# Grouped attention of a two-layer trunk: probabilities times values in float32r parts, both heads in one operand

## The chip, the core and the metric

One core of a Trainium2 chip runs the whole program. The metric is the time of one execution in microseconds on the device, lower is better. The engines are TensorE (PE, with its weight loads as PEld), VectorE (DVE), ScalarE (ACT), GpSimd (POOL, nearly unused here) and SyncE (SP), which issues the DMAs.

## The reference

The program is one inference step of a trunk of two layers, for 128 context tokens and 512 latent tokens (640 in all, five tiles of 128). Each layer has a grouped attention (8 query heads, 2 key heads), a state space branch (S5), a neighbourhood attention, gates that merge the three, and a gated MLP. The part that the change touches is the product of probabilities and values in the grouped attention:

```
s = jnp.einsum('bqgrd,bkgd->bgrqk', q_i, k).astype(jnp.float32) * scale
p = jax.nn.softmax(s, axis=-1).astype(v.dtype)
return jnp.einsum('bgrqk,bkgd->bqgrd', p, v)
```

A latent token attends to 512 latent keys and 128 cached ones (640 keys, five tiles), a context token to the 128 context keys (one tile). All of it is in float32.

## The kernel before

**Two kinds of product.** Nearly all large products are made from float32r parts: an operand x is split into hi (x rounded to float32r, by ACT) and lo (x - hi, by DVE; the helper is `split`, lines 130 and 99), and hi·hi, hi·lo and lo·hi are added up in PSUM. The weights are such a stream of hi/lo tiles (`raw`, `hi`, `lo`). A few products, among them probabilities times values, take plain float32 operands.

**Grouped attention.** `gqa` runs over four pairs of heads p; `stack` transposes the queries of the pair and splits them into `qst`; then `gqa_unit` runs for the token tiles t = 1, 2, 3, 4, 0. A unit computes the scores of both heads (`scores`, PSUM tiles `sc`: 8 products of 320 columns for t > 0), the softmax (`softmax`: on DVE the maximum `mx`, the reciprocal `rc` and the scaling of `P`; on ACT the exponential), transposes P tile by tile (`transpose_P`: up to four 128x128 transposes into one PSUM tile `tp`, copied by ACT into `PT`), and multiplies by the values (`pv`): for each key tile and head a float32 product with the 64 value columns as stationary operand and 128 probabilities columns as moving one; the two heads go into column tiles, that is output partitions 0 to 63 and 64 to 127 of one PSUM tile `y`. ACT copies `y` into `ya`. The PSUM tiles of `tp` (named `PT`, `y` or `tp` in rows) are a ring of two. A unit with t > 0 has 10 transposes and 10 such products, one with t = 0 has 2 and 2: 168 of each in a layer. The profile shows every float32 product of this kind as two records.

**What stands around it.** In the mixer of a layer the order of program text is: S5 input, S5 scan (`s5_scan`, marked as high priority, 64 dependent steps on DVE in tiles `sx` and `a`), projections, `gqa`, then a number of gate projections (`gates`; 14 items in layer 0 and 12 in layer 1, `AHEAD`), then `s5_out` in eight steps, each followed by a gate item. A step of `s5_out` needs the state after the scan: ACT copies it into `HK`, and PE multiplies (`mm<-HK,v` and `mm<-U,v`). After it come `glu` (tiles `a`), branch and output projections. A scheduler reorders this text at build time by its own estimate of times; on each engine the resulting order is fixed, and the engine executes it in that order. So the gate products (`mm<-h,hi` and `mm<-h,lo`) stand between the products of the attention. `s5_out` and the gates share a ring of two PSUM tiles `mm`, so that not more than the gates in front of a step and half a gate item behind it can be computed before that step has its state.

Lines in rows: 227 is every matmul, 230 every transpose, 130 every ACT operation, 99 every DVE operation with two tensors, 112 and 117 DVE operations with scalars, 852 and 856 the maximum and the reciprocal of the softmax.

Of the kernel before, what the change touches and what calls it, by code (L numbers as in the profile page):

```python
# [10 lines left out]
F = mybir.dt.float32  # L11
R = mybir.dt.float32r
# [38 lines left out]
class Trunk:  # L51
# [621 lines left out]
    def mixer(self, l):  # L673
        with ExitStack() as ey:
            p_y = self.pool(ey, "y")
            with ExitStack() as ek, ExitStack() as ec:
                p_z = self.pool(ek, "z")
                zt = p_z.tile([128, 5, NT], F, tag="zt", name="zt")
                va = p_z.tile([128, 6, 128], F, tag="va", name="va")
                HS = self.slot_a([128, 82, 2, 32])  # L680
                U = self.slot_v().rearrange("p a (b c) -> p a b c", c=80)
                self.run_all(self.zu(l, U))
# [85 lines left out]
    def zqkv(self, l, zt, va):  # L768
        def copy(t, dst, src):
            if t % 2:  # L770
                self.cpy(dst, src)
            else:
                self.act(dst, src)

        def ev_q(t, o):
            copy(t, zt[:, t, 0:512], o)

        def ev_kv(t, o):
            self.act(zt[:, t, 512:640], o[:, 0:128])
            copy(t, va[:, t], o[:, 128:256])  # L780
            if t == 0:
                self.dma(self.O["ga_v"][l], va[:, 0])

        self.dma(va[:, 5], self.A["cva"][l])
        return self.tm_run("zq", l, 2, 512, ev_q), self.tm_run("zkv", l, 4, 256, ev_kv)

    def nv(self, l, VN):
# [45 lines left out]
    def transpose_P(self, parts, pool, npt):  # L833

        pt = []
        for g in range(0, len(parts), 4):
            n = len(parts[g:g + 4])
            tp = self.tp("PT")
            for i, x in enumerate(parts[g:g + 4]):
                self.transpose(tp[:, i * 128:i * 128 + 128], x)  # L840
            sb = pool.tile([128, 512], F, tag="PT", name="PT", bufs=npt)
            self.act(sb[:, :n * 128], tp[:, :n * 128])
            pt.extend(sb[:, i * 128:i * 128 + 128] for i in range(n))
        return pt

    def softmax(self, P, src, nk):

# [100 lines left out]
    def gqa_unit(self, pool, p_sc, p, t, q, va):  # L948

        kv = p // 2  # L950
        k, klo = self.kst[:, kv], self.kst[:, 2 + kv]
        nk = 640 if t else 128
        qv = lambda x: x[:, t * 128:t * 128 + 128]
        sc = []
        for hh in range(2):
            sc.append(p_sc.tile([128, 1024], F, tag="sc", name="sc"))
            for a, c0, n in ((0, 128, 320), (512, 448, 320)) if t else ((0, 0, 128),):
                self.scores(sc[hh][:, a:a + n], q[:, hh], k, klo, qv, lambda x: x[:, c0:c0 + n])
        P = pool.tile([128, 2, 640], F, tag="P", name="P", bufs=2)
        self.softmax(P, [x.rearrange("p (b c) -> p b c", b=2)[:, :, :320] if t else x[:, :128] for x in sc], nk)  # L960
        pt = self.transpose_P([P[:, hh, kt * 128:kt * 128 + 128] for kt in range(nk // 128) for hh in range(2)], pool, 2)
        o = self.pv([1, 2, 3, 4, 5] if t else [0], pt, lambda vt, hh: va[:, vt, kv * 64:kv * 64 + 64])
        c = t * 128
        self.act(self.ya[:, p, c:c + 128], o[:, 0:128])


    def neighbourhood(self, l, p_na, p_y, Ga):
# [623 lines left out]
```

## Time and profile before

| What | Value |
|---|---|
| median of 3 runs | 2423.01 us (2422.66 to 2423.14) |
| the profiled execution | 2418.54 us, of which the span of the core is 2416.8 us |
| PE busy | 2334.5 us, 97% of the span |
| PE weight loads busy | 2103.6 us, 87% |
| DVE busy | 1501.8 us, 62% |
| ACT busy | 1221.7 us, 51% |
| share of PE, DMA, ACT and DVE in the chain that ended last | 85%, 4%, 4%, 3% |
| mean granted TensorE clock | 0.99 of full speed |

The busy shares are means over the whole program. Where an engine waits, and for what, is read from the stretches around the grouped attention: in layer 0 it runs from 221 to 458 us and in layer 1 from 1430 to 1673 us.

### The profile page before, as it was taken

The page shows a single profiled execution, that of the slowest core. Times are in us where ns is not written, and L with a number is a line of the kernel's source. Part 1 is how long each engine was busy: PE and PEld are TensorE (multiplying, and loading weights), DVE is VectorE, ACT ScalarE, POOL GpSimd, SP SyncE. Part 2 cuts the span into 40 slices and gives each one's busy share as a digit, 9 for nine tenths or more (in the row PEclk, how much of TensorE's full clock was granted, in tenths as well). Part 3 has the DMA queues.
Part 4 walks back from the last instruction along what each step waited for, and adds up shares of the span by engine and source line. Part 5 has one row for each costly group of instructions (what it writes and reads, how often), then busy time and mean ns, then how long its engine had stood idle before and what let it go on. Part 6 is the DMA issues. An engine that isn't in the chain of part 4 may idle for free.

```text
span 2416.8 us, 41307 instructions
## 1 busy us (share of the span) xinstructions
PE 2334.5 (97%) x16026; PEld 2103.6 (87%) x16026; DVE 1501.8 (62%) x3339; ACT 1221.7 (51%) x2657; POOL 0.7 (0%) x6
## 2 busy tenths in 40 slices
PE   5999999998999999999999999999999999999998
PEld 4899898877887899999888998888998899999886
DVE  8789647366557776665474495463775665444456
ACT  5434676336536444344364447754474564444444
POOL 0000000000000000000000000000000000000000
PEclk8999999999999999999999999999999999999999
DMA  7863242444244666654555323413321532222335
GB/s 270 276 220 98 100 147 68 161 147 132 80 157 159 204 200 208 201 173 138 170 183 186 121 81 124 138 49 124 97 64 54 176 130 71 79 72 78 114 114 174
DMA packets 160270, 334.56 MB, mean 138 GB/s; under 512 B 39434, under 2 KB 73290, under 8 KB 160074
## 3 DMA queue, kind: packets, MB, share of 16 engines
q1 hardware_dynamic: 160074, 331.92, 41.7%
q8 instruction: 126, 2.06, 0.4%
q14 instruction: 70, 0.57, 0.1%
HBM read 288.71 MB, written 52.53 MB: 141 GB/s over the span
## 4 chain that ended last, share of the span: by engine, by line
PE 85%; DMA 4%; ACT 4%; DVE 3%; issue 1%; SPq 0%; DVEq 0%; ACTq 0%
PE mm L227 49%; PE m L227 16%; PE mx L227 7%; PE tq L227 4%; PE y L227 3%; PE PT L230 2%; DMA ar<-in_wmod 2%; PE sc L227 1%; DMA raw<-in_wst 1%; ACT HK L130 1%; DVE lo L99 1%; PE BT L230 1%; ACT h L130 1%; PE E L227 1%; DMA cd<-pr 1%
## 5 line engine op out<-in xcount | busy, mean ns | idle before, releaser
L227 PE MATMUL mm<-h,hi 128*128 128x384 f32 (+1 forms) x3808 | 855.8, 313 | 6.3 <-ACT h L130 4.1
L227 PEld LDWEIGHTS mm<-h,hi 128*128 128x128 f32 x3808 | 642.7, 190 | 23.4 <-issue 12.8
L227 PE MATMUL mm<-h,lo 128*128 128x384 f32 (+1 forms) x1904 | 593.7, 312 | 0.0
L99 DVE TENSOR_TENSOR lo<-raw,hi 128x1024 fp32r<-128x1024 f32 x294 | 359.6, 1224 | 294.2 <-ACT hi L130 282.6
L130 ACT ACTIVATE hi<-raw 128x1024 fp32r<-128x1024 f32 x294 | 310.9, 1058 | 291.5 <-PE mm L227 196.6
L227 PEld LDWEIGHTS mm<-h,lo 128*128 128x128 f32 x1904 | 361.5, 190 | 5.2 <-issue 4.9
L227 PE MATMUL m<-h,hi 128*128 128x256 f32 (+1 forms) x1120 | 250.6, 312 | 2.1 <-ACT vn L130 1.1
L227 PEld LDWEIGHTS m<-h,hi 128*128 128x128 f32 x1120 | 188.7, 190 | 7.8 <-issue 4.4
L227 PE MATMUL m<-h,lo 128*128 128x256 f32 (+1 forms) x560 | 174.0, 311 | 0.1
L117 DVE SCALAR_TENSOR_TENSOR c<-u,blob,c 128x641 f32<-128x641 f32 x156 | 137.9, 884 | 2.2
L130 ACT ACTIVATE PT<-PT 128x512 f32<-128x512 f32 (+1 forms) x176 | 86.8, 498 | 93.1 <-PE PT L230 72.9
L227 PEld LDWEIGHTS m<-h,lo 128*128 128x128 f32 x560 | 106.2, 190 | 1.8 <-issue 1.4
L130 ACT ACTIVATE u<-mm 128x256 f32<-128x256 f32 (+1 forms) x156 | 48.0, 344 | 117.0 <-PE mm L227 117.0
L227 PE MATMUL mm<-a,hi 128*128 128x384 f32 (+1 forms) x384 | 89.3, 320 | 4.2 <-ACT a L130 3.1
L130 ACT ACTIVATE HK<-a 64x32 f32<-64x32 f32 (+1 forms) x256 | 77.5, 337 | 8.2 <-PE mm L227 6.2
L227 PE MATMUL mm<-hi,sph 128*128 128x512 f32 x208 | 78.6, 393 | 1.5 <-ACT sph L130 1.4
L227 PE MATMUL mm<-lo,sph 128*128 128x512 f32 x208 | 78.5, 392 | 0.0
L99 DVE TENSOR_TENSOR pr<-PW,cS 128x576 f32<-128x576 f32 x64 | 47.9, 755 | 48.3 <-PE mx L227 32.3
L227 PE MATMUL mm<-set,hi 128*128 128x384 f32 (+1 forms) x324 | 74.8, 317 | 0.5 <-DVE a L117 0.4
L227 PE MATMUL mm<-hi,spl 128*128 128x512 f32 x208 | 73.2, 393 | 0.0
L130 ACT ACTIVATE c<-u,blob 128x641 f32<-128x641 f32 x78 | 72.2, 925 | 1.9
L227 PEld LDWEIGHTS mm<-a,hi 128*128 128x128 f32 x384 | 63.9, 190 | 7.5 <-ACT a L130 4.1
(357 smaller groups left out, 4295.3 us busy)
## 6 DMA issues: line engine op xcount, KB each, us to landing
raw<-in_wst SPq DMA_DIRECT2D x308, 512.0 KB, 3.7
ar<-in_wmod SPq DMA_DIRECT2D x80, 512.0 KB, 4.0
cd<-pr SPq DMA_DIRECT2D x32, 288.0 KB, 4.4
v<-cd SPq DMA_DIRECT2D x32, 288.0 KB
wm<-in_wmod SPq DMA_DIRECT2D x8, 1024.0 KB
xd<-xt SPq DMA_DIRECT2D x15, 512.0 KB, 2.8
xt<-xd SPq DMA_DIRECT2D x15, 512.0 KB, 6.0
bd<-BT SPq DMA_DIRECT2D x28, 256.0 KB, 3.7
```

The costliest lines, as they stand in the source:

```text
L99: return self.nc.vector.tensor_tensor(out=out, in0=a, in1=b, op=op)
L117: self.nc.vector.scalar_tensor_tensor(out=out, in0=a, scalar=s, in1=b, op0=op0, op1=op1)
L130: return self.nc.scalar.activation(out=out, in_=a, func=func, **kw)
L227: return self.nc.tensor.matmul(out=out, lhsT=lhsT, rhs=rhs, start=start, stop=stop)
L230: return self.nc.tensor.transpose(out, in_, self.ident)
```

## The change

The values are kept as (hi | lo) pairs: for each token tile and key head a stationary operand of 128 columns, 64 of hi and 64 of lo. The probabilities of both heads are transposed as before, but the PSUM tile is now split into hi (ACT, in the place of the copy) and lo (DVE, new), each 128x512 (or 128x256 for the last key tile). Per key tile there are two products: the stationary operand with hi of both heads (256 columns), and the same with lo. The result has hi·p in partitions 0 to 63 and lo·p in 64 to 127; ACT copies the second half out (`yl`), and DVE adds the two halves into `ya`, once per head. The products of a group of key tiles are issued one group of transposes late. The neighbourhood attention keeps the old form.

```diff
-                va = p_z.tile([128, 6, 128], F, tag="va", name="va")
+                va = p_z.tile([128, 6, 2, 128], R, tag="va", name="va")
...
-            copy(t, va[:, t], o[:, 128:256])
+            put_v(t, o[:, 128:256])
             if t == 0:
-                self.dma(self.O["ga_v"][l], va[:, 0])
-
-        self.dma(va[:, 5], self.A["cva"][l])
+                self.act(v32, o[:, 128:256])
+                self.dma(self.O["ga_v"][l], v32)
+
+        def put_v(t, src):
+            v = src.rearrange("p (a d) -> p a d", a=2)
+            self.split(va[:, t, :, 0:64], va[:, t, :, 64:128], v)
+
+        v32, cva = (self.p_st.tile([128, 128], F, tag=x, name=x, bufs=1) for x in ("v32", "cva"))
+        self.dma(cva, self.A["cva"][l])
+        put_v(5, cva)
...
+    def pv_pair(self, P, nk, tiles, pool, v):
+        n, todo, o = nk // 128, [], None
+        def products():
+            g, m, hi, lo = todo.pop(0)
+            for i in range(m):
+                w, c = v(tiles[g + i]), slice(256 * i, 256 * i + 256)
+                self.mm(o[:, 0:256], w, hi[:, c], g + i == 0, False)
+                self.mm(o[:, 0:256], w, lo[:, c], False, g + i == n - 1)
+        for g in range(0, n, 2):
+            m = min(2, n - g)
+            tp = self.tp("PT")
+            for i in range(2 * m):
+                kt, hh = g + i // 2, i % 2
+                self.transpose(tp[:, i * 128:i * 128 + 128], P[:, hh, kt * 128:kt * 128 + 128])
+            hi, lo = (pool.tile([128, 512], R, tag=f"PT{x}", name="PT", bufs=2) for x in "hl")
+            c = slice(0, 256 * m)
+            self.split(hi[:, c], lo[:, c], tp[:, c])
+            todo.append((g, m, hi, lo))
+            if len(todo) == 2:
+                if o is None:
+                    o = self.tp("y")
+                products()
...
-        pt = self.transpose_P([P[:, hh, kt * 128:kt * 128 + 128] for kt in range(nk // 128) for hh in range(2)], pool, 2)
-        o = self.pv([1, 2, 3, 4, 5] if t else [0], pt, lambda vt, hh: va[:, vt, kv * 64:kv * 64 + 64])
-        c = t * 128
-        self.act(self.ya[:, p, c:c + 128], o[:, 0:128])
+        o = self.pv_pair(P, nk, [1, 2, 3, 4, 5] if t else [0], pool, lambda vt: va[:, vt, kv])
+        rest = pool.tile([64, 256], F, tag="yl", name="yl")
+        self.act(rest, o[64:128, 0:256])
+        for hh in range(2):
+            c = slice(hh * 128, hh * 128 + 128)
+            self.add(self.ya[hh * 64:hh * 64 + 64, p, t * 128:t * 128 + 128], o[0:64, c], rest[:, c])
```

Over the whole program PE keeps 336 products of probabilities and values (now 128x256 in place of 64x128) and all its other instructions; DVE gets 192 more instructions: 64 splits of 128x512, 40 of 128x256, 80 additions of 64x128, and 12 splits of the values in the place of 4 copies; ACT gets 8 more.

The scheduler places the new DVE work among the steps of the scan. DVE in layer 0, at the end of the scan, before the change (`a` and `sx` are the scan's state and products, `A` its coefficients, `qst` the queries of the next pair of heads):

```order
L99 TENSOR_TENSOR a<-a,sx 128x64 x2
L99 TENSOR_TENSOR sx<-a,A_245 128x64 x2
L99 TENSOR_TENSOR a<-a,sx 128x64
L117 SCALAR_TENSOR_TENSOR qst<-tp,qst 64x512
L99 TENSOR_TENSOR a<-a,sx 128x64
L117 SCALAR_TENSOR_TENSOR qst<-tp,qst 64x128
```

The same engine after the change, a little ahead of that place (unit t = 4 of the first pair; `PT<-PT` is the new split, `ya<-y,yl` the new addition):

```order
L99 TENSOR_TENSOR ya<-y,yl 64x128 x2
L99 TENSOR_TENSOR PT<-PT 128x512
L99 TENSOR_TENSOR sx<-a,A_245 128x64 x2
L99 TENSOR_TENSOR a<-a,sx 128x64 x2
L99 TENSOR_TENSOR PT<-PT 128x512
L99 TENSOR_TENSOR sx<-a,A_245 128x64 x2
L99 TENSOR_TENSOR a<-a,sx 128x64 x2
L99 TENSOR_TENSOR sx<-a,A_245 128x64 x2
L99 TENSOR_TENSOR a<-a,sx 128x64
L99 TENSOR_TENSOR PT<-PT 128x256
```

Up to the last row of the scan, DVE in layer 0 now has 8 splits of 128x512, 5 of 128x256, 10 additions and 3 more instructions for the values (five splits for two copies), and of the next pair's softmax and queries, which stood behind the scan, 2 maxima, 1 scaling, 1 reciprocal, one `qst` of 64x512 and two of 64x128. In layer 1 it has 8, 4, 6 and 3, and one more `lo<-raw,hi`.

PE in layer 0 in front of the first product with the scan's state, before the change:

```order
L230 MATMUL PT<-ident,P 128x128 x6
L227 MATMUL y<-PT,va 64x128 x10
L230 MATMUL PT<-ident,P 128x128 x2
L227 MATMUL y<-PT,va 64x128 x2
L230 MATMUL tp<-ident,zt 128x128 x5
L227 MATMUL mm<-HK,v 128x80
L227 MATMUL mm<-h,hi 128x384 x2
```

and after it:

```order
L230 MATMUL PT<-ident,P 128x128 x8
L227 MATMUL y<-PT,va 128x256 x5
L230 MATMUL PT<-ident,P 128x128 x2
L227 MATMUL y<-PT,va 128x256 x5
L230 MATMUL PT<-ident,P 128x128 x2
L227 MATMUL y<-PT,va 128x256 x2
L230 MATMUL tp<-ident,zt 128x128 x5
L227 MATMUL sc<-kst,qst 128x320 x12
L227 MATMUL mm<-HK,v 128x80
L227 MATMUL mm<-h,hi 128x384 x2
```

Twelve score products of the next pair have moved ahead of the product with `HK`; the same gate products stand in front of it as before.

## Rows read from the trace of the kernel before

**Rows 1.** The page: busy time by engine; chain that ended last, by engine

```profile
PE 2334.5 (97%) x16026; PEld 2103.6 (87%) x16026; DVE 1501.8 (62%) x3339; ACT 1221.7 (51%) x2657; POOL 0.7 (0%) x6
...
PE 85%; DMA 4%; ACT 4%; DVE 3%; issue 1%; SPq 0%; DVEq 0%; ACTq 0%
```

**Rows 2.** Windows: length; busy us of PE, PEld, DVE, ACT, POOL; clock; DMA

```profile
271.00:274.30 3.30, 3.08 (x10) 3.08 (x11) 0.51 (x2) 3.17 (x9) 0.00 (x0) 0.50 0.00 0
...
222.00:272.00 50.00, 46.76 (x364) 43.14 (x363) 42.64 (x181) 25.51 (x58) 0.00 (x0) 0.99 0.24 84
271.00:362.00 91.00, 88.83 (x695) 84.66 (x696) 39.01 (x81) 74.54 (x207) 0.00 (x0) 0.98 0.40 135
1430.00:1473.00 43.00, 42.40 (x324) 39.81 (x323) 36.61 (x149) 22.33 (x50) 0.00 (x0) 1.00 0.24 80
1473.00:1560.00 87.00, 85.13 (x678) 80.12 (x678) 31.87 (x63) 71.91 (x200) 0.00 (x0) 1.00 0.44 148
```

**Rows 3.** Timeline of PE, layer 0: start us, length us, engine, line, operation

```profile
235.16 1.09 PE L227 MATMUL y<-PT,va 128*64 128x128 f32 x16
236.18 0.62 PE L227 MATMUL mm<-h,hi 128*128 128x384 f32 x2
...
238.45 0.52 PE L227 MATMUL mm<-h,hi 128*128 128x384 f32 x2
...
238.98 0.51 PE L227 MATMUL mm<-h,hi 128*128 128x384 f32 x2
239.42 0.44 PE L227 MATMUL y<-PT,va 128*64 128x128 f32 x4
239.79 0.66 PE L230 MATMUL PT<-ident,P 128*128 128x128 f32 x4
...
241.04 0.40 PE L227 MATMUL mm<-h,hi 128*128 128x256 f32 x2
...
242.47 0.40 PE L227 MATMUL mm<-h,hi 128*128 128x256 f32 x2
```

**Rows 4.** DVE by form, 222 to 272 us: busy, mean ns, idle before, releaser

```profile
L99 DVE TENSOR_TENSOR a<-a,sx 128x64 f32<-128x64 f32 x72 | 15.8, 220 | 0.8
...
L852 DVE TENSOR_REDUCE mx<-sc 128x1 f32<-128x640 f32 x8 | 6.6, 820 | 0.7 <-PE sc L227 0.6
L99 DVE TENSOR_TENSOR lo<-raw,hi 128x1024 fp32r<-128x1024 f32 x5 | 6.1, 1223 | 2.9 <-ACT hi L130 1.8 <-PE PT L230 1.1
L112 DVE TENSOR_SCALAR P<-P,rc 128x640 f32<-128x640 f32 x8 | 4.4, 549 | 0.0
```

**Rows 5.** DVE by form, 145 to 272 us: the splits nearest to the new ones

```profile
L99 DVE TENSOR_TENSOR kst<-tq,kst 64x512 fp32r<-64x512 f32 x4 | 2.7, 685 | 0.1
...
L99 DVE TENSOR_TENSOR kst<-tq,kst 64x128 fp32r<-64x128 f32 x4 | 1.2, 288 | 0.1
...
L99 DVE TENSOR_TENSOR kst<-ropes,kst 128x256 fp32r<-128x256 f32 x1 | 0.4, 418 | 0.0
```

**Rows 6.** Timelines of PE, ACT and DVE, layer 0, around the scan's end

```profile
266.07 1.64 PE L227 MATMUL y<-PT,va 128*64 128x128 f32 x20 [1.13 <-ACT PT L130]
...
271.22 0.71 PE L227 MATMUL mm<-HK,v 128*128 128x80 f32 x2 [1.47 <-ACT HK L130]
...
270.75 6.55 ACT L130 ACTIVATE HK<-a 64x128 f32<-64x128 f32 x15
...
271.01 0.22 DVE L99 TENSOR_TENSOR a<-a,sx 128x64 f32<-128x64 f32 x1
```

**Rows 7.** Timelines of DVE and PE, layer 1, around the scan's end

```profile
1470.13 0.47 DVE L99 TENSOR_TENSOR a<-a,sx 128x64 f32<-128x64 f32 x2
...
1472.62 0.45 PE L227 MATMUL mm<-HK,v 128*128 128x80 f32 x2
```

**Rows 8.** Timeline of PE behind the scan's end: two later waits

```profile
287.00 0.85 PE L227 MATMUL sc<-kst,qst 128*128 128x320 f32 x4 [1.66 <-ACT P L130]
...
1582.74 1.01 PE L227 MATMUL mm<-a,hi 128*128 128x384 f32 x2 [2.55 <-ACT a L130]
```

More of the change, by code (lines that the diff above doesn't have):

```diff
@@ L844, in transpose_P @@
         return pt
+    def pv_pair(self, P, nk, tiles, pool, v):
[20 more added lines that the diff above has]
+                products()
+        if o is None:
+            o = self.tp("y")
+        while todo:
+            products()
+        return o
     def softmax(self, P, src, nk):
```

## The prediction, made before the run

> **What bounds the kernel now.** I read the page first. PE is busy 97% of the span and DVE 62% [rows 1]; taken alone, that says that whatever saves PE time counts in full and that DVE has room. Busy shares are means, so I then read the windows around the grouped attention. They show two regimes in each layer. From the start of the attention to the end of the scan (222 to 272 us, 1430 to 1473 us) DVE is busy 42.64 of 50 and 36.61 of 43 us, and PE 46.76 of 50 and 42.40 of 43 [rows 2]. Behind it (271 to 362, 1473 to 1560) DVE falls to 39 of 91 and 32 of 87 us while PE stays at 89 of 91 and 85 of 87 [rows 2]. So in front of the scan's end DVE is the fuller engine, and behind it PE.
>
> The timelines say what ties the two together. In layer 0 the last step of the scan starts on DVE at 271.01 us, and PE's first product with the scan's state starts at 271.22, after PE has waited 1.47 us for the copies `HK`, and 1.13 us a little earlier for `PT` with nothing else to do [rows 6]. PE's gate products ahead of that place are used up by then, since the ring of `mm` tiles allows no more. In layer 1 the scan's last step starts at 1470.13 and the product with `HK` at 1472.62 [rows 7], and PE is just fed until then. The scan's end is therefore a gate that PE passes in both layers: in layer 0 it already arrives early, in layer 1 about in time. What is put on DVE in front of the gate moves the gate; what is saved on PE in front of it is worth nothing; what is saved on PE behind it counts.
>
> **The change part by part.**
>
> *PE, products.* In the old form 16 records (four key tiles, two heads) take from 235.16 to 236.18 us, and 4 records (one key tile) from 239.42 to 239.79 [rows 3]: 1.02 and 0.37 us. That is (1.02 - 0.37)/3 = 0.217 us for a key tile and 0.15 us for the edge of a group. Entering a group costs more: three float32r products of 384 columns take 0.53 us from 238.45 to 238.98, so two take 0.353, but the last two before the group take 0.44 [rows 3]; 0.08 us. A unit with t > 0 has one group of each size: 1.02 + 0.37 + 2 × 0.08 = 1.55 us. In the new form it has ten products of 256 columns in float32r. The gate products have that shape: twelve of them go from 241.04 to 242.47 us [rows 3], 0.119 us each with their weight loads hidden, so 1.19 us. The gain is 0.36 us × 32 units = 11.5 us. A unit with t = 0 goes from 0.37 + 0.08 to 0.24: 0.21 × 8 = 1.7 us. Together 13.2 us of PE time. In both forms the first of four pairs of heads lies in front of the gate; three quarters lie behind it, 9.9 us, 5.0 us for each layer.
>
> For a key tile by itself the rows give 0.217 us in the old form and 2 × 0.119 = 0.238 in the new one: the whole gain is at the edges of the groups. The Trainium skill speaks against the change here: FP8 and Floating Point Precision (TensorE Precision Notes) says that a true float32 product takes four passes and a reduced one reads the operand once, and TensorE: Matmul & The Clock Gate (Part 3, packing small matmuls) that column tiles run at the same time. By that, a key tile is 4 × 128 columns before and 2 × 256 after, no gain at all; the rows agree within a tenth for the inside of a group. By the rule alone the 13.2 us would be zero.
>
> *DVE in front of the gate.* The order shows what now stands there. The nearest rows for the new forms are the splits of the keys: 0.685 us for 64x512, 0.418 for 128x256, 0.288 for 64x128 [rows 5]. Layer 0: 8 × 0.685 + 5 × 0.418 + 10 × 0.288 + 3 × 0.288 for the values = 11.3 us, and of the next pair, moved here from behind the scan, two maxima at 0.820, one scaling at 0.549 [rows 4], and one and two `qst` at the price of 0.685 and 0.288: 3.5 us. Together 14.8 us. Layer 1: 8 × 0.685 + 4 × 0.418 + 6 × 0.288 + 3 × 0.288 + one `lo` at 1.223 [rows 4] = 11.0 us.
>
> How far does the scan's end move? At most by all of it, plus waits: in the last units of the pair PE has no gate work left, so PE, ACT and DVE hand a tile on in turn (transposes, copy, split, product, addition), and DVE's order has four to seven scan steps of 0.2 us [rows 4] between two such hand-overs; I count some 2 us. So +17 in layer 0 and +13 in layer 1. At least by the sum less all idle time of DVE in these windows, 50 - 42.64 = 7.4 and 43 - 36.61 = 6.4 us [rows 2]: +7.4 and +4.6. About half of that idle time is waits for ACT in front of `lo` and of the softmax (2.9 + 0.7 us [rows 4]), which vanish when DVE is late; the rest is single gaps between dependent steps and stays. I take +11 us in layer 0 and +8 in layer 1.
>
> *PE at and behind the gate.* Layer 0: the gate +11; behind it -5.0 for the products, -1.8 because twelve score products (4 take about 0.6 us) now stand ahead of it, and -1.0 because the wait of 1.66 us for the next softmax at 287 [rows 8] should shrink (bounds 0 and 1.66): +3.2. Layer 1: +8 - 5.0 - 0.5 = +2.5. The clock: after PE's wait in layer 0 the granted clock is 0.50 for the 3.3 us from 271 [rows 2], the level of 1.2 GHz, which costs half of that, 1.6 us. Layer 0 has paid that already; layer 1, where PE does not wait today, would pay it new: +1.6.
>
> *Longer chains without cover.* Between the transposes and the products there is now a split on DVE of 0.69 us and a hand-over more. Where gate products stand between, it is hidden; if they were gone, each of the 96 groups that hold two or one key tiles would cost PE about 0.9 us. Cover is thin when `s5_out` is done and `glu` has not begun: there PE waits today, 2.55 us for `a` at 1582.74 [rows 8], and DVE's work for `glu` stands in the same queue as the new splits. Bounds 0 and 6 us for both layers; I take 1.0, since other units and DVE's light load lie there.
>
> *Edits with one answer.* `yl` in place of the `ya` copy and the values' split on ACT change ACT by a few us, and ACT is busy half of the span [rows 1]. The load `cva` now stands earlier at the start, ahead of loads that PE waits for; it is one tile of 128x128, and I give it nothing, beside bounds as wide as those above. The product ring `tp` is held longer, which is in the hand-overs above.
>
> Sum: 3.2 + 2.5 + 1.6 + 1.0 = +8.3 us. The profiled execution before is 2418.5 us, so it would be 2426.8; the median of the runs stands 4.5 us above that execution, and the same difference on it gives 2431.3.
>
> **The rivals.**
>
> *The gate moves little.* DVE's idle time takes up all it can: +7.4 - 5.0 - 1.8 - 1.0 and +4.6 - 5.0 - 0.5, no new stretch at 1.2 GHz, no exposed chain: -1.3 us, 2422. For it: the scan has high priority with the scheduler, and waits of several us stand in DVE's rows. Against it: those waits sit where ACT waits for PE, which stays so.
>
> *The scan is no gate at all.* If PE finds work in front of `HK` in any case, or the late scan only takes away waits that PE has now, all 13.2 us count: 2410. For it: the chain of waits gives PE 85% and DVE 3%, and PE is busy 97% [rows 1]. Against it: the order puts the same gate products in front of the product with `HK`, and PE waits there today [rows 6]. It decides for a gain as soon as the gate moves by less than the 5 us that a layer saves behind it.
>
> *The edges stay.* If entering and leaving costs because float32 transposes and float32r products alternate, and not because of the old products' form, they stay, since the transposes remain; then a key tile costs 0.02 us more, 168 × 0.02 = 3.5 us, in place of 13.2 saved. Behind the gate that is 9.9 + 2.6 us worse than my sum: 2444. This is the result of the skill's rule above. Against it: transposes next to gate products in the old order show no such entry.
>
> *The chain into `glu` is delayed.* DVE's splits wait in order in front of `glu`'s work, at its upper bound: 5 us more than my sum, 2436.
>
> **How the numbers follow.** My forecast, +8 us with a spread of +3 to +14 from the bounds of the gate, has 0.52; the gate that moves little 0.24; no gate 0.14; edges that stay 0.06; the chain into `glu` 0.04. A measurement here can tell about 0.2%, 4.8 us, from no change. Of the forecast's spread about 0.06 lies below that, so slower has 0.46 + 0.06 + 0.04 = 0.56, the same 0.24 + 0.06 = 0.30, faster 0.14. The range goes from 2417, which leaves out most of the case without a gate, to 2445, which takes in the edges that stay; without the other cases it would be 2426 to 2437.
>
> **What would show it.** Right: the scan's last `a<-a,sx` and the first `mm<-HK,v` come 7 to 17 us later in layer 0 and 5 to 13 in layer 1 against the first `sc` product; DVE nearly full until then; PE idle some 10 us in front of `HK` in both layers, with the granted clock at 0.5 behind it in layer 1 too; products `y` 0.12 us apart and no pause before or after their groups; the stretch from the first to the last `mm<-HK,v` shorter by some 4 us. Wrong: the first `HK` product at its old place, or PE busy up to it; `y` groups with pauses; or a pause of PE before `mm<-a,hi` much longer than now.

## The result and the profile after

The changed kernel takes 2438.2 us (2436.03 to 2438.68, 4 runs) against 2423.07 us (2422.66 to 2424.4, 4 runs) of the kernel before: 15.1 us more, a ratio of 1.006 with a 95% interval of 1.0042 to 1.0077. Its profiled execution took 2437.93 us, with a span of 2436.1 us.

The page of the changed kernel, busy time by engine and the chain that ended last (as [rows 1]):

```profile
PE 2341.8 (96%) x15690; PEld 2130.0 (87%) x15690; DVE 1577.2 (65%) x3531; ACT 1233.2 (51%) x2665; POOL 0.7 (0%) x6
...
PE 84%; DVE 6%; DMA 4%; ACT 4%; issue 1%; SPq 0%; DVEq 0%; ACTq 0%
```

DVE has 75 us more work, and its share of the chain has doubled. PE's busy time hardly moved, but a busy PE is also one that works at half clock, so stretches have to be read. Windows of the changed kernel in layer 0, from just behind the first scores to the first product with `HK`, around the end of the scan, and from the first to the last product with `HK` (columns as in [rows 2]):

```profile
226.40:286.10 59.70, 53.52 (x348) 50.25 (x347) 55.25 (x214) 28.36 (x63) 0.00 (x0) 0.89 0.24 80
273.50:290.30 16.80, 13.29 (x42) 10.91 (x43) 12.74 (x51) 9.42 (x23) 0.00 (x0) 0.50 0.01 3
286.10:372.50 86.40, 85.88 (x636) 84.74 (x635) 45.12 (x95) 72.84 (x199) 0.00 (x0) 0.98 0.43 142
```

In front of the gate (the end of the scan, for which PE's products with `HK` wait) DVE is busy 55 of 60 us and PE idles 6 us; and for 16.8 us around the gate the granted clock is 0.50, the level of 1.2 GHz, where the kernel before had 3.3 us of it [rows 2]. The first of these two readings in layer 1, and then its stretch at 0.50:

```profile
1447.90:1495.10 47.20, 44.90 (x299) 42.78 (x297) 42.55 (x165) 23.23 (x50) 0.00 (x0) 0.93 0.26 84
1488.30:1498.50 10.20, 9.71 (x34) 8.01 (x35) 6.78 (x31) 6.07 (x14) 0.00 (x0) 0.50 0.16 51
```

PE idles 2.3 us there, and the clock is at 0.50 for 10.2 us. Timelines of PE and DVE around the gate in layer 0:

```profile
271.46 0.63 PE L230 MATMUL PT<-ident,P 128*128 128x128 f32 x4 [2.33 <-DVE ya L99]
273.50 0.69 PE L230 MATMUL PT<-ident,P 128*128 128x128 f32 x2 [0.34 <-DVE PT L99]
277.02 1.08 PE L227 MATMUL y<-PT,va 128*128 128x256 f32 x2 [0.89 <-DVE ya L99]
279.42 0.45 PE L230 MATMUL tp<-ident,zt 128*128 128x128 f32 x1 [0.47 <-DVE ya L99]
280.56 1.43 PE L227 MATMUL sc<-kst,qst 128*128 128x320 f32 x4 [0.69 <-DVE qst L117]
286.12 0.55 PE L227 MATMUL mm<-HK,v 128*128 128x80 f32 x2
...
285.88 0.22 DVE L99 TENSOR_TENSOR a<-a,sx 128x64 f32<-128x64 f32 x1
```

The last step of the scan is at 285.88 where it was at 271.01 [rows 6]. The first score product, in the kernel before and in the changed one:

```profile
220.88 0.90 PE L227 MATMUL sc<-kst,qst 128*128 128x320 f32 x5
```

```profile
225.25 1.03 PE L227 MATMUL sc<-kst,qst 128*128 128x320 f32 x6
```

Counted from there the scan's last step comes after 60.6 us in place of 50.1. Every wait of PE in the timeline above ends with an instruction of DVE, while the waits of before in this place ended with ACT [rows 6]; one wait of the changed kernel that is not shown there, 0.94 us at 284.89 us, ends with ACT as well. In layer 1 the last two steps start at 1494.49 us:

```profile
1494.49 0.48 DVE L99 TENSOR_TENSOR a<-a,sx 128x64 f32<-128x64 f32 x2
1495.13 0.71 PE L227 MATMUL mm<-HK,v 128*128 128x80 f32 x2
```

From the first scores (1446.92, before 1430.12) to the last of them this is 47.8 us, before 40.3. PE's first product with `HK` comes 48.2 us after the first scores, before 42.5.

The new products themselves are what the sum took them for. PE in a unit of layer 0 (as [rows 3]):

```profile
238.38 0.28 PE L227 MATMUL mm<-h,hi 128*128 128x256 f32 x1
238.49 0.76 PE L227 MATMUL y<-PT,va 128*128 128x256 f32 x5
239.09 0.28 PE L227 MATMUL mm<-h,hi 128*128 128x256 f32 x1
239.21 0.28 PE L227 MATMUL mm<-h,lo 128*128 128x256 f32 x1
239.33 0.38 PE L230 MATMUL PT<-ident,P 128*128 128x128 f32 x2
```

Five products take 0.60 us, 0.120 each, and the gate product behind them follows without a pause.

**Where the time lies.** To compare kernels whose order differs I split PE's time into three. For each pair of neighbouring instructions of PE the distance of their starts is taken. The median distance of the same two kinds of instruction, at full clock and without idle time in the record, is PE's own time; what is over it is idle time where the record has some, clock where the stretch ran at half clock, and own time otherwise. Both stretches are summed: from the first `E` product of a layer to the end of its attention and value projections (106.23 to 465.43 us and 1322.76 to 1674.84 us in the trace before). The last two columns are the time from the first score product to the last step of the scan. "Before, again" is a second execution (run e4, below); for the kernels of the experiments see the next section. How much of the excess is put down to idle time and how much to the clock depends on this rule by some 2 us.

| Kernel | length | own | idle | clock | scan, layer 0 | scan, layer 1 |
|---|---|---|---|---|---|---|
| before | 711.3 | 684.7 | 21.2 | 5.4 | 50.1 | 40.3 |
| before, again (e4) | 713.9 | 684.7 | 21.6 | 7.7 | 50.1 | 40.3 |
| after | 725.4 | 669.1 | 37.1 | 19.2 | 60.6 | 47.8 |
| e1 first pair old | 720.6 | 674.1 | 36.8 | 9.7 | 47.8 | 41.7 |
| e2 first pair new | 728.6 | 679.7 | 29.2 | 19.8 | 58.7 | 49.8 |
| e5 no lo | 709.9 | 669.7 | 29.5 | 10.8 | 59.1 | 42.8 |
| e6 no add | 716.3 | 670.3 | 36.9 | 9.1 | 60.6 | 47.7 |
| e7 neither | 698.0 | 668.8 | 24.5 | 4.7 | 53.2 | 41.5 |
| e8 y late | 728.2 | 668.8 | 45.7 | 13.7 | 70.3 | 49.3 |
| e12 before, one group | 702.2 | 678.8 | 20.2 | 3.2 | 51.1 | 39.3 |

Against the mean of the two executions of before, PE saves 15.6 us of its own work in these stretches, idles 15.7 us more and loses 12.7 us more at half clock: +12.8 us. The other 2 us of the 15.1 lie outside. Each kernel of the experiments is ordered anew by the scheduler, so beside its edit it can also have other instructions in front of a place; where that matters it is said.

### The profile page after: what moved, and what is told of

Read it like the earlier page. It is cut to its first block, busy times and chain, and to the rows that moved or that the text cites. A ratio compares the mean times of both kernels' runs of the same rounds, so it can differ in the third digit from the quotient of the medians.

```text
span 2436.1 us, 40841 instructions
## 1 busy us (share of the span) xinstructions
PE 2341.8 (96%) x15690; PEld 2130.0 (87%) x15690; DVE 1577.2 (65%) x3531; ACT 1233.2 (51%) x2665; POOL 0.7 (0%) x6
## 4 chain that ended last, share of the span: by engine, by line
PE 84%; DVE 6%; DMA 4%; ACT 4%; issue 1%; SPq 0%; DVEq 0%; ACTq 0%
PE mm L227 49%; PE m L227 16%; PE mx L227 7%; PE tq L227 4%; PE y L227 2%; PE PT L230 2%; ACT HK L130 1%; DMA cd<-pr 1%; DMA ar<-in_wmod 1%; PE sc L227 1%; DMA wm<-in_wmod 1%; DVE lo L99 1%; DVE a L117 1%; PE BT L230 1%; ACT h L130 1%
## 5 line engine op out<-in xcount | busy, mean ns | idle before, releaser
L130 ACT ACTIVATE PT<-PT 128x512 fp32r<-128x512 f32 (+3 forms) x176 | 87.0, 498 | 88.0 <-PE PT L230 84.0
L227 PE MATMUL mm<-a,hi 128*128 128x256 f32 (+1 forms) x384 | 87.6, 317 | 3.2 <-DVE a L117 1.6
L227 PE MATMUL y<-PT,va 128*128 128x256 f32 x336 | 75.7, 317 | 5.1 <-DVE PT L99 2.3
L99 DVE TENSOR_TENSOR PT<-PT 128x512 fp32r<-128x512 f32 (+1 forms) x104 | 60.6, 585 | 26.9 <-ACT PT L130 26.3
```

Of the source, the lines that this page charges most:

```text
L99: return self.nc.vector.tensor_tensor(out=out, in0=a, in1=b, op=op)
L130: return self.nc.scalar.activation(out=out, in_=a, func=func, **kw)
L227: return self.nc.tensor.matmul(out=out, lhsT=lhsT, rhs=rhs, start=start, stop=stop)
```

## The experiments

**e4, the kernel before once more.** 

> The kernel before once more, for a second trace of it, since its profiled execution lies 4.5 us below its median. Expected: about 2423 us; the stretch from the first scores to the last product with HK in layer 0 (221 to 362 us) and in layer 1 (1430 to 1560) within 0.5 us of the first trace; the 4.5 us lie in waits for DMAs, at the start or between 470 and 640 us.

One execution, 2427.76 us. The expectation was wrong by half: layer 0 differs too, by 3.3 us behind the gate (from the first to the last product with `HK`). Windows of the same instructions, in the first trace and in this one:

```profile
285.00:288.00 3.00, 1.34 (x11) 1.14 (x10) 1.46 (x4) 2.96 (x10) 0.00 (x0) 1.00 0.00 0
288.00:292.00 4.00, 4.00 (x36) 4.00 (x35) 3.80 (x8) 3.63 (x11) 0.00 (x0) 1.00 0.34 123
```

```profile
285.80:288.80 3.00, 1.34 (x11) 1.14 (x10) 1.46 (x4) 2.96 (x10) 0.00 (x0) 1.00 0.00 0
288.80:292.80 4.00, 4.00 (x22) 4.00 (x21) 3.61 (x7) 3.16 (x8) 0.00 (x0) 0.53 0.34 123
```

The first line of each is the same to the last digit: PE idles 1.66 of 3 us. Behind it one execution goes on at full clock and does 36 products in 4 us, the other at half clock and does 22. So a wait of PE has a second price, which falls due in some executions and not in others, and a single trace of this kernel is worth some 4 us either way. The first trace, on which the prediction rests, was a lucky one.

**e1, the first pair of heads in the old form.**

```diff
...
+        if p == 0:
+            pt = self.transpose_P([P[:, hh, kt * 128:kt * 128 + 128] for kt in range(nk // 128) for hh in range(2)], pool, 2)
+            o = self.pv([1, 2, 3, 4, 5] if t else [0], pt, lambda vt, hh: self.vf[:, vt, kv * 64:kv * 64 + 64])
+            c = t * 128
+            self.act(self.ya[:, p, c:c + 128], o[:, 0:128])
+            return
         o = self.pv_pair(P, nk, [1, 2, 3, 4, 5] if t else [0], pool, lambda vt: va[:, vt, kv])
```

> The first pair of heads (p = 0, the one whose units stand in front of the end of the scan) gets the old form back (float32 products in column tiles, copy of y by ScalarE); pairs 1 to 3 keep the new form, and the values are kept in both forms (five more copies on ScalarE in each layer). Theory A, the gate: what the change lost is VectorE's new work in front of the end of the scan. Then the last scan step comes some 10 us earlier in layer 0 and 6 to 8 in layer 1 against the changed kernel, the stretch at half clock in front of the first product with HK shrinks from 17 to 3 us, and what the pairs 1 to 3 save behind it stays: 2438 - 16 = 2422 us (2417 to 2427). Rival B: the new form costs behind the gate (longer chains from transposes to products, the product ring), so three quarters of the loss stay: 2434 us or more.

2432.33 us (2430.54 to 2433.82) against 2425.59 of the kernel before, ratio 1.0028 (1.0017 to 1.0039). The gate did what theory A said: the scan's last step comes 47.8 us after the first scores in layer 0, earlier than in the kernel before, and 41.7 us in layer 1. (In layer 1 the first product with `HK` still comes at 48.7 us, since the order puts more gate products in front of it; PE waits only 2 us there.) But of 16 us only about 8 came back, and PE idles as much as in the changed kernel (36.8 us in the table). It idles elsewhere. 2.5 us are the run's own: ahead of the first scores PE waits 1.4 and 3.2 us for the second form of the values (`vf`), where it waits 0.9 and 1.2 us for `va` in the changed kernel. Windows of the 23 us behind the last product with `HK`, where `glu` begins, in layers 0 and 1; first the kernel before, then the changed kernel, then e1:

```profile
362.00:385.00 23.00, 21.60 (x162) 17.08 (x162) 15.26 (x27) 17.54 (x36) 0.00 (x0) 1.00 0.31 73
1560.00:1583.00 23.00, 17.93 (x128) 13.65 (x128) 17.11 (x36) 17.27 (x34) 0.00 (x0) 0.97 0.29 72
```

```profile
372.50:395.50 23.00, 18.82 (x105) 16.52 (x105) 20.40 (x42) 17.44 (x36) 0.00 (x0) 0.93 0.31 72
1580.70:1603.70 23.00, 17.42 (x107) 14.69 (x106) 21.09 (x42) 16.80 (x32) 0.00 (x0) 1.00 0.29 72
```

```profile
355.00:378.00 23.00, 16.57 (x97) 13.12 (x96) 21.19 (x39) 15.54 (x30) 0.00 (x0) 1.00 0.28 73
1571.50:1594.50 23.00, 16.47 (x96) 12.96 (x95) 21.19 (x40) 15.56 (x31) 0.00 (x0) 1.00 0.28 72
```

DVE goes from 15 and 17 us to 20 and 21 of 23, and PE from 21.6 and 17.9 to 18.8 and 17.4, in e1 to 16.6 and 16.5: there is a second stretch in each layer in which DVE is the fuller engine. PE's timeline in e1 names the waits:

```profile
367.86 0.62 PE L227 MATMUL mm<-a,hi 128*128 128x384 f32 x2 [1.28 <-DVE a L117]
...
369.19 0.86 PE L227 MATMUL y<-PT,va 128*128 128x256 f32 x5 [0.37 <-DVE PT L99]
...
373.68 0.63 PE L230 MATMUL PT<-ident,P 128*128 128x128 f32 x4 [0.46 <-DVE ya L99]
375.04 0.86 PE L227 MATMUL y<-PT,va 128*128 128x256 f32 x5 [0.73 <-DVE PT L99]
```

`glu`'s own work (`a`), the splits and the additions queue on DVE for each other. Theory A is half of the truth, and rival B the other half.

There is a third place, and there DVE is not full: the last units of the attention, in e1 in both layers, in the changed kernel in layer 1. A window and two lines of PE of the changed kernel:

```profile
1664.00:1672.60 8.60, 6.99 (x35) 5.49 (x36) 5.09 (x17) 4.97 (x14) 0.00 (x0) 0.80 0.00 0
```

```profile
1663.99 0.44 PE L230 MATMUL PT<-ident,P 128*128 128x128 f32 x2 [0.34 <-DVE PT L99]
...
1667.88 0.63 PE L230 MATMUL PT<-ident,P 128*128 128x128 f32 x4 [0.99 <-DVE ya L99]
```

Only transposes, scores and products `y` follow each other here, with no other product between them, and PE waits at the hand-overs although DVE is busy 5.09 of 8.60 us. That is the chain without cover of the prediction, and not a full queue.

**e2, only the first pair in the new form** (the condition of e1 turned round, `if p:`). 

> The mirror of the run before: only the first pair of heads has the new form, pairs 1 to 3 the old one. Theory A: the whole price of the gate is paid (+10 us in layer 0, +6 in layer 1), some us ahead of the attention too for the splits of the values, and nothing is saved behind the gate: 2423 + 4 + 16 less the waits that vanish behind a late gate, 2438 us (2433 to 2444). Rival B, the cost lies behind the gate: 2423 to 2428 us.

2437.78 us (2434.72 to 2439.56) against 2425.59, ratio 1.0049 (1.0036 to 1.0063): 12 us slower with a quarter of the products, as theory A has it. Together, e1 and e2 cost 6.7 + 12.2 = 18.9 us against 15.1 of the whole change. Both runs carry the second form of the values, whose waits are 2.5 us longer than those for `va` in each of them (see e1), which is more than the 3.8 us over: the price in front of the gate and the one behind it seem to add up.

**e3, the buffer of the modulation weights in a space of its own.**

```diff
-                    raw = lambda k: p_na.tile([128, 1024], F, tag="ar", name="ar", bufs=1)
+                    raw = lambda k: self.p_st.tile([128, 1024], F, tag="ar", name="ar", bufs=1)
```

> The changed kernel, with one edit: the buffer `ar`, into which the modulation weights of the next layer are loaded, gets a space of its own in place of one in the pool that is opened behind the attention. In the trace after, TensorE waits 5.04 us for the first of these loads at 484.84 us, and that load is issued only at 479.99 us, behind the last products of the attention at 477.03; in the kernel before the last products are at 457.39, the issue is at 457.74, and the wait is 1.09 us. Theory C: the load waits until the attention has left the space, and the attention ends 20 us later, so the wait goes with the edit: 2438 - 5 = 2433 us (2431 to 2435), and about a tenth of the wait is left. Rival D: the load is late for its place in the queue behind the weight loads, or the next of these loads takes over the wait: 2437 to 2439 us.

2438.99 us (2432.46 to 2442.28) against 2425.59, ratio 1.0051 (1.0036 to 1.0066), so no gain can be shown. PE's products with `ar`, first in the changed kernel, then in e3:

```profile
490.26 1.08 PE L227 MATMUL m<-ar,scv 128*32 128x256 f32 x8 [5.04 <-DMA ar<-in_wmod]
```

```profile
480.10 0.63 PE L227 MATMUL m<-ar,scv 128*32 128x256 f32 x6
...
488.73 1.08 PE L227 MATMUL m<-ar,scv 128*32 128x256 f32 x8 [4.39 <-DMA ar<-in_wmod]
```

A load of the same stream is still waited for, 4.39 us in place of 5.04. Theory C falls, as rival D said. The expectation had the wrong load: the wait of 5.04 us is not for the first one but for the second, between the products of 484.58 and those of 490.26, and the second is issued at 485.27 us, when the products with the first have read the only buffer. In e3 the first load is issued at 0.74 us, and the second, at 484.37, still comes behind the products with the first.

**e5, no split of the probabilities.**

```diff
-            hi, lo = (pool.tile([128, 512], R, tag=f"PT{x}", name="PT", bufs=2) for x in "hl")
+            hi = lo = pool.tile([128, 512], R, tag="PTh", name="PT", bufs=2)
             c = slice(0, 256 * m)
-            self.split(hi[:, c], lo[:, c], tp[:, c])
+            self.act(hi[:, c], tp[:, c])
```

> The changed kernel without the 104 splits `lo` of the probabilities on VectorE: both products of a key tile use the hi part, so TensorE has the same instructions and the result lacks the low parts of the probabilities (this part of the computation is left out). From the first runs: in the two attention layers TensorE's own work is 15.5 us shorter in the changed kernel than before, its waits are 16 us longer and its losses at half clock some 13 us larger, and giving the first pair the old form back moved the waits behind the end of the scan in place of removing them. Theory A2: the split on VectorE, which stands between the transposes and the products of a unit and holds the PSUM tile, makes these waits. Then they go almost wholly, with most of the half clock: 2438 - 16 - 8 = 2414 us (2410 to 2422). Rival E: it is the additions into ya, which hold the tile y of the same ring of two; then at most a third goes: 2431 us or more.

2412.46 us (2407.77 to 2415.73) against 2424.5, ratio 0.9953 (0.9936 to 0.9969): theory A2 was right on the time. It was not on the place: in layer 0 the scan still ends 59.1 us after the first scores. Some 7.6 us of splits are gone in front of it and it ends 1.5 us earlier; in part that is because the scheduler now puts two more maxima and one more scaling of the next pair there (2.2 us), and what holds the rest is not shown. (The second product of a key tile takes the hi part again, so the result has it twice in place of hi and lo; PE's work is the same.)

**e6, no additions.**

```diff
-        rest = pool.tile([64, 256], F, tag="yl", name="yl")
-        self.act(rest, o[64:128, 0:256])
         for hh in range(2):
             c = slice(hh * 128, hh * 128 + 128)
-            self.add(self.ya[hh * 64:hh * 64 + 64, p, t * 128:t * 128 + 128], o[0:64, c], rest[:, c])
+            self.act(self.ya[hh * 64:hh * 64 + 64, p, t * 128:t * 128 + 128], o[0:64, c])
```

> The changed kernel without the 80 additions on VectorE: ScalarE copies the hi halves of y into ya (two copies of 64x128 in place of one of 64x256), and the halves with the low parts of the values are left out of the result. The splits of the probabilities stay. Rival E, the ring held by the additions: TensorE's waits on ya (2.3 + 0.9 + 0.5 us in front of the product with HK, about 1 us at some places behind it in each layer) go, with the half clock that they cause: 2438 - 8 - 8 = 2422 us (2416 to 2428). Theory A2, the split: the splits still hold the ring, 2432 to 2437 us.

2429.93 us (2422.55 to 2434.07) against 2424.5, ratio 1.0022 (1.0011 to 1.0034). Between the two: the additions cost some 10 of the 15 us, though the splits still hold the gate at 60.6 us.

**e7, both edits.** 

> Both of the two runs above in one: neither splits of the probabilities nor additions on VectorE (the low parts of probabilities and values are left out of the result); TensorE's instructions are those of the changed kernel. It shows what the products alone give. If VectorE's new work is the whole loss: 2425 - 15 = 2410 us (2406 to 2416). If the new products or the longer order themselves cost (rival B'): 2418 us or more.

2408.57 us (2403.97 to 2410.91) against 2424.5, ratio 0.9934 (0.9919 to 0.9949): 15.9 us faster, which is PE's own saving of the table (684.7 - 668.8 = 15.9). Idle time and clock are back at 24.5 and 4.7 us, and the gate in layer 0 at 53.2. So the products are worth 15.9 us, DVE's splits of the probabilities and its additions cost 31 us, and the change is the difference. Taken one at a time, the splits cost 21 (e6 against e7) to 27 us (after against e5), the additions 4 (e5 against e7) to 10 (after against e6).

**e8, the tile `y` taken late** (a loop over all groups of transposes first, then `o = self.tp("y")` and all products; three buffers for hi and lo). 

> The changed kernel with the products of a unit issued behind all its transposes, as in the old form, so that the tile y takes its place in the ring of two only when the last PT tile is transposed (three buffers in place of two for hi and lo). No instruction more or less. In the changed kernel y is taken at the second group, and the remaining groups of transposes share one PSUM tile. If that is what makes the waits (rival F): about half of the 16 us of waits and of the half clock go, 2438 - 12 = 2426 us (2420 to 2431). If splits and additions themselves are late (theories A2 and E): 2436 to 2442 us.

2436.58 us (2435.64 to 2437.06) against 2424.5, ratio 1.0052 (1.0037 to 1.0066). By its time rival F falls: PE idles more than in the changed kernel (45.7 us), and the scan in layer 0 ends 70.3 us after the first scores. But the run does not isolate the ring of two. With the new order the scheduler also put more in front of the scan's end in layer 0 (12 splits of 128x512 in place of 8, 18 maxima in place of 12, with what belongs to them some 12 us of DVE's work), and the scan ends 9.7 us later than in the changed kernel. PE still waits for `ya`, 5.3 us in layer 0. That taking `y` late cures nothing is shown; whether a ring of three would is not.

**e9 and e10, part of DVE's other work on GpSimd**, in the changed kernel and in the kernel before.

```diff
...
-                    self.split(hi, lo, self.raw_t.pop(i))
+                    raw = self.raw_t.pop(i)
+                    if self.on_pool:
+                        self.act(hi, raw)
+                        self.nc.gpsimd.tensor_tensor(out=lo, in0=raw, in1=hi.bitcast(F), op=ALU.subtract)
+                    else:
+                        self.split(hi, lo, raw)
...
```

> The changed kernel, all its arithmetic kept, with 62 of VectorE's splits `lo<-raw,hi` of the weights (31 in each layer, those of the stretch from the attention to the branch projections, 1.22 us each on VectorE) given to GpSimd, which has nothing to do there. Theory A2: the loss is that the new splits and additions queue on VectorE behind its other work; with 76 us less of that work they are done in time, the end of the scan comes as early as in the kernel before, and most of the 30 us that the new work costs come back: 2412 us (2406 to 2420). Rival G: what costs is the longer chain itself (transposes, ScalarE, VectorE, products), however free VectorE is: 2430 us or more. Rival H: GpSimd is too slow for the weights, and TensorE waits for `lo` in front of the products with the weights: slower than 2440 us. No row so far shows GpSimd at such an operation.

> The same 62 splits of the weights on GpSimd in the kernel before, as the control of the run above: there the end of the scan waits for VectorE too. Expected: TensorE's waits in front of the product with HK in layer 0 go (1.5 us and 1.1 us, with 3.4 us at half clock behind them), and little else, since TensorE has no room to gain behind it: 2420 us (2415 to 2425); with a slow GpSimd the same loss as in the run above.

2472.81 us and 2455.93 us against 2423.83, ratios 1.0205 (1.0188 to 1.0221) and 1.0126 (1.0109 to 1.0143). Groups of POOL over the whole of e10 and of DVE from 222 to 272 us in it, then DVE's group in the same stretch of the kernel before:

```profile
L199 POOL TENSOR_TENSOR lo<-raw,hi 128x1024 fp32r<-128x1024 f32 x62 | 154.6, 2494 | 1522.2 <-ACT hi L130 1481.2 <-DMA out_ssm<-a 10.5 <-PE mm L232 10.3
...
L99 DVE TENSOR_TENSOR sx<-a,A 128x64 f32<-128x64 f32 x74 | 21.9, 337 | 0.9
L99 DVE TENSOR_TENSOR a<-a,sx 128x64 f32<-128x64 f32 x74 | 18.3, 248 | 1.0
```

```profile
L99 DVE TENSOR_TENSOR sx<-a,A 128x64 f32<-128x64 f32 x72 | 13.0, 221 | 0.9
```

A split that DVE does in 1.22 us takes GpSimd 2.49 us, and the mean of the steps of the scan goes from 221 to 337 and from 220 to 248 ns. The mean hides what happens. POOL and DVE in e10 around one of the splits:

```profile
260.32 2.39 POOL L199 TENSOR_TENSOR lo<-raw,hi 128x1024 fp32r<-128x1024 f32 x1 [7.93 <-ACT hi L130]
...
259.64 0.36 DVE L99 TENSOR_TENSOR sx<-a,A 128x64 f32<-128x64 f32 x2
...
260.43 2.50 DVE L99 TENSOR_TENSOR sx<-a,A 128x64 f32<-128x64 f32 x2
```

Between 222 and 272 us there are five splits on POOL, and five steps of the scan, one beside each, take 2.29 to 2.45 us; every other step keeps its 0.2 us. So a step that meets a split stands about as long as the split takes, and DVE gains nothing by giving the split away. Not every operation stands: the maxima `mx<-sc` that run beside a split in e10 keep their 0.82 us.

The scan's end is not where e10 loses: it comes 47.1 us after the first scores in layer 0 and 42.8 in layer 1, against 50.1 and 40.3. Most of PE's new idle time lies ahead of the first scores, where waits for DVE and ACT are new. Windows from the first `E` product to the first scores in layers 0 and 1, in the kernel before and in e10:

```profile
106.23:220.88 114.65, 114.17 (x1017) 105.63 (x1017) 93.72 (x240) 50.60 (x150) 0.00 (x0) 1.00 0.60 188
1322.76:1430.12 107.36, 107.03 (x875) 100.18 (x874) 69.54 (x218) 46.84 (x139) 0.00 (x0) 1.00 0.35 114
```

```profile
105.13:226.43 121.30, 111.34 (x950) 100.41 (x950) 103.83 (x239) 48.08 (x145) 29.84 (x11) 0.96 0.56 175
1347.24:1455.40 108.16, 99.21 (x811) 90.89 (x811) 69.93 (x200) 44.12 (x134) 32.23 (x13) 1.00 0.34 109
```

PE idles 10.0 and 9.0 us there in place of 0.5 and 0.3. Rival H had the time of e9 right (over 2440 us) but not the wait: no wait of PE ends with POOL. And the pair says nothing on A2 against G, since DVE was not relieved. The question whether a freer DVE would be enough is answered by e5 to e7 only in so far as the work is gone, not moved.

**e11, probabilities rounded only.**

```diff
...
-            hi, lo = (pool.tile([128, 512], R, tag=f"PT{x}", name="PT", bufs=2) for x in "hl")
-            c = slice(0, 256 * m)
-            self.split(hi[:, c], lo[:, c], tp[:, c])
...
+            hi = pool.tile([128, 512], R, tag="PTh", name="PT", bufs=3)
+            self.act(hi[:, 0:256 * m], tp[:, 0:256 * m])
+            todo.append((g, m, hi))
+        o = self.tp("y")
+        for g, m, hi in todo:
+            for i in range(m):
+                self.mm(o[:, 0:256], v(tiles[g + i]), hi[:, 256 * i:256 * i + 256], g + i == 0, g + i == n - 1)
```

> The changed kernel with the probabilities only rounded to float32r: ScalarE's copy of the transposed tile is their hi part, VectorE has no split of them, and each key tile has one product of 256 columns with (v hi | v lo) in place of two; products of a unit behind all its transposes. The low part of the probabilities is left out of the result. It takes 168 products of 0.119 us from TensorE, 20 us, beside the splits, whose loss was 26 us: 2412 - 20 = 2392 us (2387 to 2402) if TensorE's time counts in full; 2405 us or more if the additions on VectorE still set the pace.

2400.01 us (2396.3 to 2408.23) against 2423.83, ratio 0.9907 (0.9888 to 0.9926): the fastest of all, with the attention at one rounding to float32r. Over e5 the missing products brought 12 of their 20 us (2412.46 to 2400.01). The other 8 were lost; the additions in front of the gate are still there, and in layer 0 the scan ends 62.1 us after the first scores, but that they took the 8 us is not shown.

**e12, the kernel before with one group of products for a unit.**

```diff
-            self.act(sb[:, :n * 128], tp[:, :n * 128])
+            self.last_pt = self.act(sb[:, :n * 128], tp[:, :n * 128])
...
-        pt = self.transpose_P([P[:, hh, kt * 128:kt * 128 + 128] for kt in range(nk // 128) for hh in range(2)], pool, 2)
-        o = self.pv([1, 2, 3, 4, 5] if t else [0], pt, lambda vt, hh: va[:, vt, kv * 64:kv * 64 + 64])
+        pt = self.transpose_P([P[:, hh, kt * 128:kt * 128 + 128] for kt in range(nk // 128) for hh in range(2)], pool, 3)
+        with self.tc.issue_after(self.last_pt.ins):
+            o = self.pv([1, 2, 3, 4, 5] if t else [0], pt, lambda vt, hh: va[:, vt, kv * 64:kv * 64 + 64])
```

> The kernel before with one edit of order: the products of a unit are issued behind the copy of its last PT tile (three buffers PT in place of two), so that its ten products stand in one group in place of eight and two: 48 groups of them in place of 70 over both layers. No instruction more or less, nothing new on VectorE. If the old form loses at the edges of groups, as the sum of the prediction had it (0.15 us at the end of one, 0.08 at its start), TensorE's own work falls by 22 x 0.23 = 5 us and the time from 2424 to 2419 us (2414 to 2422), without the price that the changed kernel pays on VectorE. If the products now wait for the last copy without other work to stand between, or the edges cost nothing: 2424 us or more, with TensorE's work in the attention as before.

2413.09 us (2411.69 to 2415.55) against 2423.97, ratio 0.9955 (0.9941 to 0.9969): 10.9 us faster than the kernel before, with all of its arithmetic, and 25 us faster than the changed kernel. PE in one unit of layer 0:

```profile
322.37 1.31 PE L227 MATMUL y<-PT,va 128*64 128x128 f32 x20
323.61 0.44 PE L230 MATMUL PT<-ident,P 128*128 128x128 f32 x2
```

Twenty records take 1.24 us where 16 and 4 took 1.02 and 0.37 [rows 3]. PE's own time falls by 5.9 us (684.7 to 678.8), as 22 edges of 0.23 us say. The rest, about 5 us, lies in idle time and clock (23.4 us against 26.6 and 29.3) and outside of the attention; how much of that is the edit and how much the chance of e4 is open.

## Why the prediction was right, and what it missed

The direction and the range held: slower, 2438.2 in 2417 to 2445. The size did not: +8.3 forecast, +15.1 measured, one us above the forecast's own spread of 2426 to 2437. So the range held by luck: its upper part was there for the rival in which the edges stay, and that rival fell.

- **Products, -13.2 us.** Right, 15.6 measured in the changed kernel and 15.9 gained in e7. That the gain lies at the edges of groups is shown by e12, which removes 22 of them in the old form. The rival in which the edges stay fell with e7. The Trainium skill's count of passes for float32 (FP8 and Floating Point Precision, TensorE Precision Notes), weighed in the prediction, gave no gain; the rows agree with it for the inside of a group only (0.217 us for a key tile before, 2 × 0.120 after).
- **The gate, +11 and +8 us.** Right: +10.5 and +7.5 us from the first scores to the scan's last step, and +10.5 and +5.7 to PE's first product with `HK`. Both rivals that denied it (a gate that moves little, no gate) fell. One sign did not come: PE was to idle some 10 us in front of `HK` in both layers, and it idles 6.2 and 2.3; much of the delay is work at half clock, which has its own term below. And the gate is not the one cause: with it back at its old place (e1) nearly half of the loss stayed, 6.7 of 15.1 us.
- **The clock, +1.6 us.** The term that failed most. PE waits several times in front of the gate, and the clock stays at 0.50 through 16.8 us there in layer 0 and 10.2 us in layer 1; 12.7 us more than before are lost to it in both attention stretches, some 2 of which can be chance by the two traces of before. I had counted one stretch of 3.3 us and taken layer 0's as paid already.
- **Longer chains without cover, +1.0 us of at most 6.** Also too small. I named the place, where `s5_out` is done and `glu` begins, and looked there at PE's wait only, not at DVE's share: it was at 17 of 23 us in layer 1 already, and the splits filled it. At the attention's end the chain itself is bare, with DVE at 5.09 of 8.60 us. e1 shows the size: it idles PE 15 us longer than before though its gate is early, 4.6 us of which are its own waits for `vf`. The rival of the chain into `glu`, to which I gave 0.04 and 5 us, is thus no rival but a part of the result. The "light load" of DVE behind the gate (39 of 91 us) was again a mean.
- **The values' splits ahead of the attention, nothing.** Their place was not looked at. In the changed kernel's timeline PE waits there for DVE twice, the second time for `va`:

```profile
148.94 0.64 PE L227 MATMUL tq<-pr,bz 128*32 128x128 f32 x8 [1.42 <-DVE pr L99]
...
150.47 1.01 PE L227 MATMUL mm<-h,hi 128*128 128x384 f32 x2 [0.89 <-DVE va L99]
```

  The stretch from the first `E` product to the first scores is 117.1 us long there, and 114.7 and 114.9 in the two traces of before. But e3, e7 and e8 have the same splits and the wait for `va` too (0.8 to 0.9 us), and there the stretch is 114.2 to 114.7 us long. So a price of the values' splits is not shown.
- **The two sides together.** The sum said that DVE's work takes back 21.5 us of idle time, clock and spent savings; e7 against the changed kernel says 31.

## What to carry to other kernels

An engine at 62% can still set the pace. Before moving work to it, add the new work to its busy time stretch by stretch: in layer 0 the scan's stretch was at 42.64 of 50 us and went to 55.25 of 59.70, and the start of `glu`, at 15.26 of 23 and so hardly fuller than the mean, went to 20.40. Curing one of these places left the wait at the next. And look for stretches where nothing else stands between the links of a chain: there a link more is paid even by an engine that is not full. Price a wait of TensorE with what the clock does behind it, as a chance and not as a certainty. And where a change gains at the edges of groups, ask first whether the old instructions can simply stand in larger groups: e12 did that with one dependency and a buffer, and nothing had to be paid on another engine.

## What the runs showed of the hardware that I had not expected

- The same program, after the same wait of 1.66 us, went on at a granted clock of 1.00 in one execution and 0.53 in the next; the profiled executions of the kernel before lie 9 us apart, 2418.54 and 2427.76.
- A split of 128x1024 on GpSimd takes 2.49 us (1.22 on DVE). A step of the scan on DVE (128x64, 0.22 us) that meets such a split takes 2.29 to 2.45 us, while the maxima beside one keep their 0.82 us (e10).
- Twenty float32 records into column tiles take 1.24 us in one group, 16 take 1.02: 0.22 us for a key tile, as [rows 3] had it, so a group costs 0.15 us beside its key tiles, whatever its length.
